# Hybrid decoder layer on one core: the mask selection operand is made once for all groups and reloaded, squares are added on VectorE, B is copied ahead of the masks, z is evaluated in pairs, the tap norm gets a lower priority

## Chip, cores and metric

The kernel runs on one core of a Trainium2 chip. The metric is the device time of one execution in microseconds (us). Before the change it is 1996.78 us, the median of three runs (1994.49 to 1999.12).

## The reference, cut to what matters

One layer with D_MODEL = 1024, SEQ = 1024, BATCH = 1, all in float32. The change touches the state-space branch (SSD) and the way the taps of the convolution branch are normalised:

```python
u = h @ w_in                         # -> GLU | z | x, B, C | dt | gate_a | gate_b
y_a = silu(layer_norm(causal_dwconv(a * sigmoid(g), 31 taps))) @ w_conv_out
...
# SSD: 32 heads in 4 groups of 8, head size 64, state 128, chunks of L = 128
a_cs = cumsum(dt * a_head)                           # within a chunk
decay = exp(a_cs[l] - a_cs[s]) where l >= s          # per head
cb = C @ B^T                                         # per group and chunk
y_diag = (cb * decay) @ (x * dt)
states, prev = scan over chunks of B^T @ (decay_states * x * dt)
y = y_diag + exp(a_cs) * (C @ prev) + x * d_skip
yg = y * silu(z)
y_b = yg * rsqrt(mean(yg^2 over the group)) * norm_w @ w_ssm_out
...
h = LN(alpha*h + (sigmoid(gate_a)*y_a + sigmoid(gate_b)*y_b) @ w_o)
h = LN(alpha*h + ConvFFN(h))
```

## The kernel before

Every large product is done with three TensorE (PE) products of 128x512 in the fp32r type (lines 187 to 189, `mm3`): each operand is split into a rounded part and a rest, ScalarE (ACT) writes the first and VectorE (DVE) the second (`weights`, lines 163 and 164; `split_to`, lines 203 and 204). SyncE (SP) issues the loads of the weights, GpSimd (POOL) issues some of the other DMAs. The sequence is worked on in two halves of 512 positions (`hh` = 0, 1); each goes through `mixers` and `combine`, then comes the output projection, and the ConvFFN follows for both.

`mixers` runs over the four SSD groups `g`. For a group it projects the columns of B, C and x, and passes each through `conv4` (line 429: three multiply-adds on DVE). Then it finishes the norm of the group before (`done`), projects two pairs of GLU columns, and calls `ssd_group`. `conv31` gets a low priority: its 30 multiply-adds of 128x512 for each of 8 channel tiles (line 474, `c`) are the filler that the planner puts between other work on DVE.

`ssd_group` runs over four chunks `c`. In a chunk PE makes `px` (x transposed, line 520) and `pb` (B transposed, line 523, and C times B, line 524, in one bank). POOL makes `au` (line 526), the differences' moving operand, 128 x (8 heads x 128): `seg_mv` of the chunk times the 0/1 choice `head_of` of the group's heads. PE makes the 8 masks' exponents with `seg_st` as weights and `au` as moving operand in two banks `pg` (line 535), ACT turns them into masks `m` (lines 543, 544), DVE multiplies them by `cbm` (line 558). `po` (line 563) is the part from the state, `pn` (line 567) the state's increment from `bt` (B transposed, copied by ACT in line 557) and `xsd`; DVE updates the state (lines 571, 574); `py` (line 577) is the part within the chunk. These banks, named `sm` in the profile, rotate through four; seven are taken in a chunk, so that a `pg` takes a bank which an earlier product's reader must have freed. The projections use four other banks, `acc`.

After the chunks, `z_gate` projects z in four tiles, ACT evaluates Silu on each; DVE forms y (lines 592, 596); ACT squares it, POOL adds the squares into `ss` (line 602). `normed` then sums them on PE (`pick`, line 607), takes the root (line 612) and the reciprocal (line 613), sends the row through DRAM (POOL DMAs, lines 615 and 616) and multiplies y by it (line 619), and splits it into `yT`.

`combine` projects the second gate and the second half of the SSD output (weights `w_gb`, `w_sp`) in turn, and beside them normalises the taps: loads `cc` from `c_scr`, adds them on POOL into `mean` (line 705), PE averages over partitions (line 707), and so on until `sT`, which the projection `w_co` needs. This stands under `tc.high_priority(offset=900)`.

The order on each engine is fixed when the kernel is built: a planner lays all instructions out on a timeline of its own, by priority (`tc.high_priority`) and by its own estimates of durations, and each engine then runs its list strictly in that order. An edit of one line so moves the instructions of all engines around it. `au`, `m`, `bt`, `xs`, `xsd` have one buffer each.

Of the kernel before, what the change touches and what calls it, by code (L numbers as in the profile page):

```python
# [8 lines left out]
F32 = mybir.dt.float32  # L9
F32R = mybir.dt.float32r  # L10
AF = mybir.ActivationFunctionType
ALU = mybir.AluOpType
# [42 lines left out]
def kernel(  # L55
# [30 lines left out]
    def bank(which):  # L86
        n_ps[0] += 1
        pl, tag = (pacc, "acc") if which else (psm, "sm")
        return pl.tile([P, 512], F32, tag=tag, name=f"{tag}{n_ps[0]}")
# [22 lines left out]
        axis=AX.X,  # L112
        op=ALU.add,
    )
    kind = const.tile([P, 4], F32, name="kind")
    V.tensor_reduce(
        out=kind, in_=ident.rearrange("p (g k h) -> p k g h", k=4, h=8), axis=AX.XY, op=ALU.add
# [34 lines left out]
    c_scr = [dram.tile([8, P, HALF], F32, name=f"c_scr{i}") for i in range(2)]  # L152
    g_scr = [dram.tile([8, P, HALF], F32, name=f"g_scr{i}") for i in range(2)]
    e_scr = [dram.tile([P, HALF], F32, name=f"e_scr{i}") for i in range(2)]
    r_scr = [dram.tile([GROUPS, HALF], F32, name=f"r_scr{i}") for i in range(2)]
    y_scr = [dram.tile([8, P, HALF], F32, name=f"y_scr{i}") for i in range(2)]

# [33 lines left out]
    def project(ps, w, xs):  # L191
        for k in range(KD):
            mm3(
                ps,
                lambda i: w[:, i, k * P : (k + 1) * P],
                lambda i: xs[:, i, k, :],
                k == 0,
                k == KD - 1,
            )
# [285 lines left out]
    def z_gate(pl, hh, hT, g):  # L485

        zs = []
        for i in range(4):
            ps = bank(1)
            project(ps, weights(wz[4 * g + i], f"z{hh}_{g}_{i}"), hT)  # L490
            z = pl.tile([P, HALF], F32, tag="zs", bufs=5, name=f"zs{hh}_{g}_{i}")
            A.activation(out=z, in_=ps, func=AF.Silu)
            zs.append(z)
        return zs

    def ssd_group(pl, hh, g, xT, BT, CT, gate):
        S = states[g]
        h8 = slice(8 * g, 8 * g + 8)
        acc = pl.tile([P, 4, HALF], F32, tag="ys", name=f"ys{hh}_{g}")
        ev = e_scr[hh].rearrange("(g k i j) t -> g k j i t", k=4, j=2, i=4)  # L500
        for j in range(2):
            G.dma_start(acc[j * HP : (j + 1) * HP], ev[g, 0, j].partition_broadcast(HP))

        def heads(t):
            return t.rearrange("p (h q) -> p h q", h=8)

        def per_head(t):
            return t.unsqueeze(2).to_broadcast([P, 8, HP])

        def by_tile(t):  # L510
            return t.rearrange("p (i t) -> p i t", i=4)

        for c in range(4):
            nm = f"{hh}_{g}_{c}"
            cs = slice(c * P, (c + 1) * P)
            first = hh == 0 and c == 0
            last = hh == 1 and c == 3
            px = bank(0)
            for i in range(4):
                TE.transpose(px[:, i * P : (i + 1) * P], xT[i][:, cs], ident)  # L520
            pb = bank(0)
            if not last:
                TE.transpose(pb[:, :P], BT[:, cs], ident)
            TE.matmul(pb[:, P : 2 * P], BT[:, cs], CT[:, cs], start=True, stop=True)
            au = pl.tile([P, 8, P], F32R, tag="au", name=f"au{nm}")
            G.tensor_tensor(  # L526
                out=au,
                in0=seg_mv[:, c, :].unsqueeze(1).to_broadcast([P, 8, P]),
                in1=head_of[:, g, :].unsqueeze(2).to_broadcast([P, 8, P]),
                op=ALU.mult,  # L530
            )
            m = pl.tile([P, 8, P], F32, tag="m", name=f"m{nm}")
            for q in range(2):
                pg = bank(0)
                TE.matmul(  # L535
                    pg,
                    seg_st[:, c, :],
                    au[:, 4 * q : 4 * q + 4, :].rearrange("p h l -> p (h l)"),
                    start=True,
                    stop=True,  # L540
                )
                mq = m[:, 4 * q : 4 * q + 4, :].rearrange("p h l -> p (h l)")
                A.activation(out=mq, in_=pg, func=AF.Relu)
                A.activation(out=mq, in_=mq, func=AF.Exp, scale=-1.0)
            cbm = pl.tile([P, P], F32, tag="cbm", name=f"cbm{nm}")
            V.tensor_mul(cbm, pb[:, P : 2 * P], upper)
            xs = pl.tile([P, HALF], F32, tag="xs", name=f"xs{nm}")
            V.tensor_tensor(
                out=heads(xs), in0=heads(px), in1=per_head(dts[0][:, c, h8]), op=ALU.mult
            )  # L550
            if not last:
                xsd = pl.tile([P, HALF], F32, tag="xsd", name=f"xsd{nm}")
                V.tensor_tensor(
                    out=heads(xsd), in0=heads(px), in1=per_head(dts[1][:, c, h8]), op=ALU.mult
                )
                bt = pl.tile([P, P], F32, tag="bt", name=f"bt{nm}")
                A.copy(bt, pb[:, :P])
            V.tensor_tensor(out=m, in0=m, in1=cbm.unsqueeze(1).to_broadcast([P, 8, P]), op=ALU.mult)  # L558
            if not first:
                po = bank(0)  # L560
                for i in range(4):
                    ts = slice(i * P, (i + 1) * P)
                    TE.matmul(po[:, ts], S[:, ts], CT[:, cs], start=True, stop=True)
                V.tensor_tensor(out=acc[:, :, cs], in0=by_tile(po), in1=acc[:, :, cs], op=ALU.mult)
            if not last:
                pn = bank(0)
                TE.matmul(pn, bt, xsd, start=True, stop=True)
                if first:
                    V.tensor_copy(S, pn)
                else:  # L570
                    V.tensor_tensor(
                        out=heads(S), in0=heads(S), in1=per_head(edc[:, 1, c, h8]), op=ALU.mult
                    )
                    V.tensor_add(S, S, pn)
            py = bank(0)
            for h in range(8):
                TE.matmul(
                    py[h % 2 * HP : (h % 2 + 1) * HP, h // 2 * P : (h // 2 + 1) * P],
                    xs[:, h * HP : (h + 1) * HP],
                    m[:, h, :],  # L580
                    start=True,
                    stop=True,
                )
            if first:
                A.copy(acc[:, :, cs], by_tile(py))
            else:
                V.tensor_tensor(out=acc[:, :, cs], in0=acc[:, :, cs], in1=by_tile(py), op=ALU.add)
        zs = gate()
        ss = pl.tile([P, HALF], F32, tag="ss", name=f"ss{hh}_{g}")
        for i, y in enumerate(xT):  # L590
            k = 4 * g + i
            V.scalar_tensor_tensor(
                out=y, in0=y, scalar=nskip[:, 1, k : k + 1], in1=acc[:, i, :],
                op0=ALU.mult, op1=ALU.add,
            )
            V.tensor_mul(y, y, zs[i])
            if i == 0:
                A.activation(out=ss, in_=y, func=AF.Square)
            else:
                sq = pl.tile([P, HALF], F32, tag="yo", bufs=2, name=f"sq{hh}_{g}_{i}")  # L600
                A.activation(out=sq, in_=y, func=AF.Square)
                G.tensor_add(ss, ss, sq)

        def normed(yT):
            pm = bank(0)
            for c in range(4):
                TE.matmul(
                    pm[:4, :P], pick[:, c, :], ss[:, c * P : (c + 1) * P],
                    start=c == 0, stop=c == 3,
                )  # L610
            r = pl.tile([4, P], F32, tag="rr", name=f"rr{hh}_{g}")
            A.activation(out=r, in_=pm[:4, :P], func=AF.Sqrt, bias=eps[:4], scale=1.0 / HALF)
            V.reciprocal(out=r, in_=r)
            rd = r_scr[hh][g]
            G.dma_start(rd.rearrange("(c t) -> c t", c=4), r)
            G.dma_start(ss, rd.partition_broadcast(P))
            for i, y in enumerate(xT):
                k = 4 * g + i
                V.scalar_tensor_tensor(  # L619
                    out=y, in0=y, scalar=nskip[:, 0, k : k + 1], in1=ss,  # L620
                    op0=ALU.mult, op1=ALU.mult,
                )
                split_to(yT, (g % 2) * 4 + i, y)

        return normed
# [40 lines left out]
    def combine(hh, hT, yT):  # L666

        with pool(f"comb{hh}") as pl:
# [11 lines left out]
            for j in range(8):  # L680
# [8 lines left out]
                V.tensor_add(m, ya, ps)  # L689
                V.tensor_mul(m, m, gb)  # L690
                mb.append(m)
            with tc.high_priority(offset=900):
                cs = []
                for i in range(8):
                    c = pl.tile([P, HALF], F32, tag=f"c{i}", name=f"cc{hh}_{i}")
# [652 lines left out]
```

## Time and profile before

| what | value |
|---|---|
| median of three runs | 1996.78 us |
| the profiled execution's own time | 1997.45 us |
| its span, first to last instruction | 1995.7 us |
| mean granted TensorE clock | 0.997 |
| stage `mixers`, half 0 | about 80 to 516 us of the span |
| stage `combine`, half 0 | about 516 to 660 us |
| stage `mixers`, half 1 | about 750 to 1180 us |
| stage `combine`, half 1 | about 1180 to 1310 us |
| ConvFFN | about 1310 us to the end |

The profile's page gives busy time by engine, the span in 40 slices, the chain of work that ended last, and groups of instructions. In a group's row stand the line, the engine, the operation, the tiles as written<-read, the shape, the count, then the busy time in us and the mean ns of one, then the idle time of its engine just before them and what ended it. A "wait" of PE is idle time between two of its matmuls, put down to what released it.

### The profile page before, as it was taken

To read this page: it belongs to the slowest core of one execution; us is meant where nothing else is said; L and a number is where in the kernel's file an instruction comes from. 1 tells how busy PE (TensorE), PEld (TensorE's weight loads), DVE (VectorE), ACT (ScalarE), POOL (GpSimd) and SP (SyncE) were. 2 spreads that over 40 slices of the span, in tenths; PEclk is the share of its full clock that TensorE was granted. 3 is DMA by queue.
4 is the path that set the end of the run, shared out by engine and by line. 5 is a ranking of instruction groups with operands and counts; after the bars stand their busy time and mean duration, and the time that the engine had idled before them with its cause. 6 is when DMAs were issued, how large, how long until landed. Compare 5 with 4: busy or idle time off the path is not lost.

```text
span 1995.7 us, 24843 instructions
## 1 busy us (share of the span) xinstructions
PE 1947.5 (98%) x9240; PEld 1592.9 (80%) x9240; DVE 1701.1 (85%) x2230; ACT 1052.9 (53%) x1483; POOL 237.4 (12%) x201
## 2 busy tenths in 40 slices
PE   7999999999999999999999999999999999999998
PEld 6887777877788887788777878887878888888886
DVE  7899999989565879999999967578998888778768
ACT  5566767454453266667654646256554544553442
POOL 1112121101400001111210132001000000011000
PEclk9999999999999999999999999999999999999999
DMA  6324232523544642324243354476443232268573
GB/s 218 111 65 121 73 117 79 164 81 115 175 127 155 240 140 77 102 84 117 80 132 116 100 185 127 132 279 241 170 148 116 101 113 104 102 215 272 181 248 111
DMA packets 99241, 281.15 MB, mean 141 GB/s; under 512 B 11728, under 2 KB 11760, under 8 KB 99120
## 3 DMA queue, kind: packets, MB, share of 16 engines
q1 hardware_dynamic: 87840, 244.68, 36.9%
q0 software_dynamic: 8976, 30.69, 5.1%
q10 hardware_dynamic: 2304, 4.20, 0.6%
q8 instruction: 72, 1.18, 0.2%
q14 instruction: 49, 0.40, 0.1%
HBM read 229.44 MB, written 50.09 MB: 140 GB/s over the span
## 4 chain that ended last, share of the span: by engine, by line
PE 64%; DVE 27%; issue 5%; DMA 2%; ACT 1%; POOL 1%; SPq 0%; DVEq 0%; POOLq 0%; ACTq 0%
PE acc L189 16%; PE acc L187 16%; PE acc L188 16%; DVE c L474 11%; PE sm L187 3%; PE sm L189 3%; PE sm L188 3%; DVE xbc L429 2%; DVE w_c L164 1%; PE acc L411 1%; DVE w_z L164 1%; DMA ss<-r_scr 1%; DVE m L558 1%; DVE xbc L619 1%; POOL mean L705 1%
## 5 line engine op out<-in xcount | busy, mean ns | idle before, releaser
L474 DVE SCALAR_TENSOR_TENSOR c<-v,pc,c 128x512 f32<-128x512 f32 x480 | 385.2, 832 | 5.5 <-ACT c L463 4.3
L187 PE MATMUL acc<-hT,w_c 128*128 128x512 f32 x352 | 141.6, 402 | 0.0
L189 PE MATMUL acc<-hT,w_c 128*128 128x512 f32 x352 | 138.5, 394 | 0.0
L188 PE MATMUL acc<-hT,w_c 128*128 128x512 f32 x352 | 137.9, 392 | 0.0
L526 POOL TENSOR_TENSOR au<-seg_mv,head_of 128x1024 fp32r<-128x1024 f32 x32 | 79.8, 2494 | 374.0 <-PE sm L535 373.9
L429 DVE SCALAR_TENSOR_TENSOR xbc<-u,pc,xbc 128x512 f32<-128x512 f32 x144 | 112.3, 794 | 0.5 <-ACT xbc L427 0.4
L987 DVE SCALAR_TENSOR_TENSOR fo<-u,pc,fo 128x1024 f32<-128x1024 f32 x88 | 111.4, 1286 | 0.4 <-ACT fo L983 0.4
L187 PE MATMUL acc<-h1s,w_s 128*128 128x512 f32 x264 | 103.5, 392 | 2.3 <-ACT u L971 2.3
L188 PE MATMUL acc<-hT,w_z 128*128 128x512 f32 x256 | 103.7, 405 | 0.0
L189 PE MATMUL acc<-h1s,w_s 128*128 128x512 f32 x264 | 103.0, 390 | 0.0
L188 PE MATMUL acc<-h1s,w_s 128*128 128x512 f32 x264 | 102.7, 389 | 0.0
L187 PE MATMUL acc<-hT,w_z 128*128 128x512 f32 x256 | 101.7, 397 | 0.0
L189 PE MATMUL acc<-hT,w_z 128*128 128x512 f32 x256 | 101.6, 397 | 0.0
L1126 ACT CAST w_dn<-dr 128x1024 fp32r<-128x1024 f32 (+1 forms) x73 | 61.0, 843 | 69.8 <-DVE dr L1056 33.3
L1127 DVE TENSOR_TENSOR w_dn<-dr,w_dn 128x1024 fp32r<-128x1024 f32 (+1 forms) x73 | 70.1, 968 | 13.5 <-ACT w_dn L1126 13.2
L188 PEld LDWEIGHTS acc<-hT,w_c 128*128 128x128 f32 x352 | 66.1, 188 | 15.7 <-issue 2.4
L187 PEld LDWEIGHTS acc<-hT,w_c 128*128 128x128 f32 x352 | 66.2, 188 | 15.3 <-issue 2.4
L189 PEld LDWEIGHTS acc<-hT,w_c 128*128 128x128 f32 x352 | 66.1, 188 | 14.5 <-issue 0.8
L163 ACT CAST w_c<-st_c 128x1024 fp32r<-128x1024 f32 x48 | 50.2, 1045 | 51.6 <-PE acc L189 32.5
L187 PE MATMUL sm<-h1b,w_s 128*128 128x512 f32 x176 | 69.1, 393 | 0.0
L188 PE MATMUL sm<-h1b,w_s 128*128 128x512 f32 x176 | 69.0, 392 | 0.0
L189 PE MATMUL sm<-h1b,w_s 128*128 128x512 f32 x176 | 69.0, 392 | 0.0
(372 smaller groups left out, 5708.3 us busy)
## 6 DMA issues: line engine op xcount, KB each, us to landing
st_c<-wcol SPq DMA_DIRECT2D x50, 512.0 KB, 3.5
st_z<-wz SPq DMA_DIRECT2D x32, 512.0 KB, 3.4
st_wo<-wo SPq DMA_DIRECT2D x24, 512.0 KB, 4.1
ra<-wup SPq DMA_DIRECT2D x22, 512.0 KB, 3.5
rb<-wup SPq DMA_DIRECT2D x22, 512.0 KB, 3.5
t_scr<-fo POOLq DMA_DIRECT2D x22, 512.0 KB, 3.4
dr<-t_scr SPq DMA_DIRECT2D x44, 256.0 KB, 3.8
dr<-wdown SPq DMA_DIRECT2D x38, 256.0 KB, 4.5
```

Source lines behind the costliest of these rows:

```text
L163: A.copy(w[:, 0, :], st)
L164: (eng or V).tensor_tensor(out=w[:, 1, :], in0=st, in1=w[:, 0, :].bitcast(F32), op=ALU.subtract)
L187: TE.matmul(ps, wa(0), xa(0), start=start, stop=False, skip_group_check=more)
L188: TE.matmul(ps, wa(0), xa(1), start=False, stop=False, skip_group_check=more)
L189: TE.matmul(ps, wa(1), xa(0), start=False, stop=stop, skip_group_check=more)
L411: TE.matmul(ps[:, ts], w[:, i, k * P : (k + 1) * P], hT[:, j, k, ts], start=n == 0 and k == 0, stop=n == 2 and k == KD - 1,)
L429: V.scalar_tensor_tensor(out=o, in0=u[:, k : k + HALF], scalar=pc[:, wc + k : wc + k + 1], in1=o, op0=ALU.mult, op1=ALU.add,)
L474: V.scalar_tensor_tensor(out=accs[i], in0=v[:, k : k + HALF], scalar=pc[:, wc + k : wc + k + 1], in1=accs[i], op0=ALU.mult, op1=ALU.add,)
L526: G.tensor_tensor(out=au, in0=seg_mv[:, c, :].unsqueeze(1).to_broadcast([P, 8, P]), in1=head_of[:, g, :].unsqueeze(2).to_broadcast([P, 8, P]),
L987: V.scalar_tensor_tensor(out=o, in0=u[:, k : k + T], scalar=pc[:, wc + k : wc + k + 1], in1=o, op0=ALU.mult, op1=ALU.add,)
L1126: A.copy(w[:, 0, cs], src)
L1127: V.tensor_tensor(out=w[:, 1, cs], in0=src, in1=w[:, 0, cs].bitcast(F32), op=ALU.subtract)
```

## The change

Five edits, all in `mixers` and `combine`. A tile `lanes` holds two sums of the 0/1 choice: `head_all` (which of the 8 heads in any group) and `group_of` (which group). `au` is now made with `head_all`, which is the same for all groups, so POOL makes it for group 0 alone and writes it to DRAM (`au_scr`); the three other groups load it. The choice of the group moves into the weights: ACT makes `sg` from `seg_st` and `group_of`, and PE uses `sg` where it used `seg_st`. `bt` is copied right after B's transposition, before C times B is written to the same bank. The adds into `ss` go to DVE. z's projections are evaluated two at a time. The tap norm's priority goes from 900 to 300.

```diff
+    lanes = statep.tile([P, 16], F32, name="lanes")
+    head_all, group_of = lanes[:, :8], lanes[:, 8:12]
+    V.tensor_reduce(
+        out=head_all, in_=head_of.rearrange("p g h -> p h g"), axis=AX.X, op=ALU.add
+    )
+    V.tensor_reduce(out=group_of, in_=head_of, axis=AX.X, op=ALU.add)
...
+    au_scr = [
+        [dram.tile([P, 8 * P], F32R, name=f"au_scr{i}_{c}") for c in range(4)] for i in range(2)
+    ]
...
-        for i in range(4):
-            ps = bank(1)
-            project(ps, weights(wz[4 * g + i], f"z{hh}_{g}_{i}"), hT)
-            z = pl.tile([P, HALF], F32, tag="zs", bufs=5, name=f"zs{hh}_{g}_{i}")
-            A.activation(out=z, in_=ps, func=AF.Silu)
-            zs.append(z)
+        for i in range(0, 4, 2):
+            pss = [bank(1) for _ in range(2)]
+            for k, ps in enumerate(pss):
+                project(ps, weights(wz[4 * g + i + k], f"z{hh}_{g}_{i + k}"), hT)
+            for k, ps in enumerate(pss):
+                z = pl.tile([P, HALF], F32, tag="zs", bufs=5, name=f"zs{hh}_{g}_{i + k}")
+                A.activation(out=z, in_=ps, func=AF.Silu)
+                zs.append(z)
...
                 TE.transpose(pb[:, :P], BT[:, cs], ident)
+                bt = pl.tile([P, P], F32, tag="bt", name=f"bt{nm}")
+                A.copy(bt, pb[:, :P])
             TE.matmul(pb[:, P : 2 * P], BT[:, cs], CT[:, cs], start=True, stop=True)
             au = pl.tile([P, 8, P], F32R, tag="au", name=f"au{nm}")
-            G.tensor_tensor(
-                out=au,
-                in0=seg_mv[:, c, :].unsqueeze(1).to_broadcast([P, 8, P]),
-                in1=head_of[:, g, :].unsqueeze(2).to_broadcast([P, 8, P]),
-                op=ALU.mult,
-            )
+            if g == 0:
+                G.tensor_tensor(
+                    out=au,
+                    in0=seg_mv[:, c, :].unsqueeze(1).to_broadcast([P, 8, P]),
+                    in1=head_all.unsqueeze(2).to_broadcast([P, 8, P]),
+                    op=ALU.mult,
+                )
+                G.dma_start(au_scr[hh][c], au.rearrange("p h l -> p (h l)"))
+            else:
+                G.dma_start(au.rearrange("p h l -> p (h l)"), au_scr[hh][c])
+            sg = pl.tile([P, P], F32R, tag="sg", name=f"sg{nm}")
+            A.mul(sg, seg_st[:, c, :].bitcast(F32), group_of[:, g : g + 1])
...
-                    seg_st[:, c, :],
+                    sg,
...
-                bt = pl.tile([P, P], F32, tag="bt", name=f"bt{nm}")
-                A.copy(bt, pb[:, :P])
...
                 A.activation(out=sq, in_=y, func=AF.Square)
-                G.tensor_add(ss, ss, sq)
+                V.tensor_add(ss, ss, sq)
...
-            with tc.high_priority(offset=900):
+            with tc.high_priority(offset=300):
```

The lists of the engines move from the middle of `mixers` to the end of `combine` in both halves; behind `combine` of half 1 they are as before. Three places follow. In the names of tiles stand the half, the group and the chunk (`au0_2_2` is half 0, group 2, chunk 2); line numbers of the changed kernel are larger by 9 to 17.

PE, half 0, group 2, from the last product of chunk 1 to the first masks' exponents of chunk 2, before:

```order
L577 MATMUL sm119_2519<-m0_2_1_2491,xs0_2_1_2502 64x128 x8
L520 MATMUL sm120_2529<-ident_75,xbc0_8_2154 128x128
L520 MATMUL sm120_2529<-ident_75,xbc0_9_2194 128x128
L520 MATMUL sm120_2529<-ident_75,xbc0_10_2234 128x128
L520 MATMUL sm120_2529<-ident_75,xbc0_11_2274 128x128
L523 MATMUL sm121_2534<-ident_75,xbc0_18_2074 128x128
L524 MATMUL sm121_2534<-xbc0_22_2114,xbc0_18_2074 128x128
L535 MATMUL sm122_2540<-au0_2_2_2537,seg_st_137 128x512
```

The same place in the changed kernel:

```order
L594 MATMUL sm119_2554<-m0_2_1_2528,xs0_2_1_2539 64x128 x8
L531 MATMUL sm120_2564<-ident_75,xbc0_8_2185 128x128
L531 MATMUL sm120_2564<-ident_75,xbc0_9_2225 128x128
L531 MATMUL sm120_2564<-ident_75,xbc0_10_2265 128x128
L531 MATMUL sm120_2564<-ident_75,xbc0_11_2305 128x128
L534 MATMUL sm121_2569<-ident_75,xbc0_18_2105 128x128
L554 MATMUL sm122_2579<-au0_2_2_2574,sg0_2_2_2576 128x512
```

C times B has left this block. It comes 20 projection matmuls later, just ahead of the second masks' exponents (here with the projection row before it and the row after it):

```order
L198 MATMUL acc143_3077<-hT0_214,w_c0_31_3080 128x512
L537 MATMUL sm121_2569<-xbc0_22_2145,xbc0_18_2105 128x128
L554 MATMUL sm123_2583<-au0_2_2_2574,sg0_2_2_2576 128x512
L196 MATMUL acc143_3077<-hT0_214,w_c0_31_3080 128x512
L197 MATMUL acc143_3077<-hT0_214,w_c0_31_3080 128x512
```

So between the transposition of B and C times B there is now the time in which ACT copies `bt`.

POOL, half 0, from the norm's two DMAs of group 0 to the end of group 1, before (`au` is made by POOL, `ss` added by POOL):

```order
L615 DMA r_scr0_199<-rr0_0_1493 4x128
L616 DMA ss0_0_1162<-r_scr0_199 128x512
L526 TENSOR_TENSOR au0_1_1_1694<-seg_mv_136,head_of_104 128x1024
L526 TENSOR_TENSOR au0_1_2_1742<-seg_mv_136,head_of_104 128x1024
L526 TENSOR_TENSOR au0_1_3_1790<-seg_mv_136,head_of_104 128x1024
L526 TENSOR_TENSOR au0_2_0_2448<-seg_mv_136,head_of_104 128x1024
L502 DMA ys0_2_2437<-e_scr0_197 64x4x512 x2
L602 TENSOR_TENSOR ss0_1_1958<-ss0_1_1958,sq0_1_1_1964 128x512
```

The same stretch in the changed kernel:

```order
L632 DMA r_scr0_210<-rr0_0_1516 4x128
L633 DMA ss0_0_1185<-r_scr0_210 128x512
L548 DMA au0_1_1_1721<-au_scr0_1_203 128x1024
L548 DMA au0_1_2_1771<-au_scr0_2_204 128x1024
L548 DMA au0_1_3_1821<-au_scr0_3_205 128x1024
L548 DMA au0_2_0_2481<-au_scr0_0_202 128x1024
L513 DMA ys0_2_2468<-e_scr0_200 64x4x512 x2
```

Loads stand where products stood, in the same places of the list, and the adds are gone from it.

PE, half 0, the sum of squares of the last group, before (among the last projections of `mixers`):

```order
L187 MATMUL acc196_4151<-hT0_203,w_gt0_7_4154 128x512
L188 MATMUL acc196_4151<-hT0_203,w_gt0_7_4154 128x512
L607 MATMUL sm190_3964<-ss0_3_3813,pick_117 4x128 x4
L189 MATMUL acc196_4151<-hT0_203,w_gt0_7_4154 128x512
L187 MATMUL acc196_4151<-hT0_203,w_gt0_7_4154 128x512
```

In the changed kernel, between the first two gate projections of `combine`:

```order
L197 MATMUL acc197_4235<-hT0_214,w_gb0_0_4238 128x512
L198 MATMUL acc197_4235<-hT0_214,w_gb0_0_4238 128x512
L624 MATMUL sm190_4011<-ss0_3_3860,pick_120 4x128 x4
L196 MATMUL acc198_4267<-hT0_214,w_gb0_1_4270 128x512
L197 MATMUL acc198_4267<-hT0_214,w_gb0_1_4270 128x512
```

The sum stands 43 projection matmuls later. The product `w_sp0_0`, the first that needs this group's `yT`, is cut in two there: 12 matmuls on the half of `yT` that is already there, the 24 of `w_gb0_2`, then the other 12. Between the sum and these other 12 stand 60 matmuls of 128x512 now; before, 67 and the first 12 of `w_sp0_0` stood between. In half 1 it is 54 now, 59 before.

## The prediction

> **What bounds the kernel now.** First the page: busy times, then the 40 slices, then the chain that ended last.
>
> ```profile
> span 1995.7 us, 24843 instructions
> PE 1947.5 (98%) x9240; PEld 1592.9 (80%) x9240; DVE 1701.1 (85%) x2230; ACT 1052.9 (53%) x1483; POOL 237.4 (12%) x201
> PE   7999999999999999999999999999999999999998
> DVE  7899999989565879999999967578998888778768
> PE 64%; DVE 27%; issue 5%; DMA 2%; ACT 1%; POOL 1%; SPq 0%; DVEq 0%; POOLq 0%; ACTq 0%
> ```
>
> PE is busy nearly throughout, and in slices 3 to 8 and 16 to 23, the two `mixers`, DVE is full as well. The chain alternates between these two. How much PE can gain at all is read by stage (busy us of PE, PEld, DVE, ACT, POOL in each stretch):
>
> ```profile
> 80.00:516.00 436.00, 427.01 (x2128) 342.65 (x2127) 418.22 (x547) 260.48 (x386) 64.36 (x42) 1.00 0.33 103
> 516.00:660.00 144.00, 140.48 (x609) 114.84 (x609) 88.58 (x110) 56.64 (x72) 21.60 (x14) 0.99 0.52 171
> 750.00:1180.00 430.00, 422.48 (x2122) 341.17 (x2121) 418.29 (x544) 252.57 (x349) 69.21 (x41) 1.00 0.34 104
> 1180.00:1310.00 130.00, 128.94 (x565) 105.53 (x564) 80.05 (x96) 59.66 (x75) 22.51 (x14) 1.00 0.49 157
> 1550.00:1600.00 50.00, 50.00 (x221) 41.15 (x220) 42.85 (x50) 24.28 (x29) 1.61 (x3) 1.00 0.31 111
> ```
>
> The last row is ConvFFN, where PE never waits: 50.00 / 221 = 0.226 us for each 128x512 matmul, the unit for distances below. PE idles 9.0 + 7.5 = 16.5 us in the `mixers` and 3.5 + 1.1 = 4.6 us in `combine`. The change adds and removes no matmul, so some 21 us, 1.1%, is all that it can win. What PE waits for there:
>
> ```profile
> PE sm L535 <- DVE state L574: 5.3, 5, 1.7
> PE sm L707 <- POOL mean L705: 4.6, 2, 3.5
> PE sm L567 <- ACT bt L557: 4.1, 3, 1.8
> PE acc L189 <- DVE w_ga L164: 2.4, 1, 2.4
> PE sm L535 <- DVE state L569: 1.6, 1, 1.6
> PE sm L563 <- DVE xsd L553: 1.5, 1, 1.5
> PE acc L189 <- DVE w_so L164: 1.3, 1, 1.3
> ```
>
> Without `mean` these are 5.3 + 4.1 + 2.4 + 1.6 + 1.5 + 1.3 = 16.2 us, the 16.5 of the windows. All but `bt` name a DVE that came late.
>
> **POOL's adds and products, taken away.** POOL makes `au` only for group 0 (8 of 32) and adds no squares. What POOL's work costs DVE shows where they meet:
>
> ```profile
> L474 DVE SCALAR_TENSOR_TENSOR c<-v,pc,c x480: 641/741/2391, 76.2 to 1163.9; 128x512 f32<-128x512 f32 x160
> L474 DVE SCALAR_TENSOR_TENSOR c<-v,pc,c 128x512 f32<-128x512 f32 x480 | 385.2, 832 | 5.5 <-ACT c L463 4.3
> L526 POOL TENSOR_TENSOR au<-seg_mv,head_of 128x1024 fp32r<-128x1024 f32 x32 | 79.8, 2494 | 374.0 <-PE sm L535 373.9
> L602 POOL TENSOR_TENSOR ss<-ss,sq 128x512 f32<-128x512 f32 x24 | 41.1, 1712 | 93.5 <-ACT sq L601 92.4
> 98.14 1.40 DVE L474 SCALAR_TENSOR_TENSOR c<-v,pc,c 128x512 f32<-128x512 f32 x2
> 100.60 3.05 DVE L474 SCALAR_TENSOR_TENSOR c<-v,pc,c 128x512 f32<-128x512 f32 x2
> 100.27 2.17 POOL L526 TENSOR_TENSOR au<-seg_mv,head_of 128x1024 fp32r<-128x1024 f32 x1 [14.62 <-PE sm L535]
> ```
>
> The same two multiply-adds take 1.40 us alone and 3.05 beside an `au`. Over all, line 474's mean of 832 ns stands over a median of 741: 480 x 0.091 = 43.7 us lost in this line alone, beside 79.8 + 41.1 = 120.9 us of these two POOL groups. Removed are 24/32 x 79.8 + 41.1 = 101 us of them, so at least 43.7 x 101/120.9 = 36 us of DVE come back. The Trainium skill ("SBUF — State Buffer", Who interferes with whom) says that a VectorE instruction with two inputs in SBUF and a reading GpSimd instruction exclude each other for a whole instruction; by it up to 101 us would come back, the trace says some 36, and the time below is the same by both, since PE is what it can free.
>
> DVE takes over 24 adds of 128x512 in SBUF, priced by line 596, the same form:
>
> ```profile
> L596 DVE TENSOR_TENSOR xbc<-xbc,zs 128x512 f32<-128x512 f32 x32 | 20.7, 699 | 0.0
> L557 ACT COPY bt<-sm x28: 242/266/274, 87.3 to 1118.7; 128x128 f32<-128x128 f32 x28
> ```
>
> 24 x 0.70 = 17 us. Each add now waits on DVE for ACT's square, with DVE's list behind it; weight splits and taps stand between in the new list, so I take no wait, and 24 x 0.63 = 15 us if ACT's square is always just being made. DVE's balance is -36 + 17 = -19 us of 836 us (-4 at the worst), a little more than the 16.5 us by which PE was kept waiting. The two small sums for `lanes` lie in the start, before x arrives.
>
> **New order of a chunk.** `pg` takes the bank that the state's increment of the chunk before held (DVE line 574 frees it). From `pn` to the next `pg` the old lists leave 3.9 us at least (counting matmuls in units of 0.226), five times under 6; the new ones 7.8 at least. `bt` is copied ahead of the masks instead of behind them, so its 4.1 us go; in exchange C times B now waits for that copy: 20 matmuls, 4.5 us, for a copy of 0.27 us on an ACT that is 60% busy (260.48 of 436). From the second `pg` to `py`, the room for masks, it is 7.9 us at least now, 7.3 before, and mostly 2 us more than before. From the transpositions to `pn`, the room for xs and xsd, it is 5.4 us at least and mostly 1 us less than before. What that takes:
>
> ```profile
> 109.45 0.66 PE L520 MATMUL sm<-ident,xbc 128*128 128x128 f32 x4
> 112.82 0.67 DVE L553 TENSOR_TENSOR xsd<-sm,wds 128x512 f32<-128x512 f32 x1
> ```
>
> 113.49 - 110.11 = 3.4 us with a full DVE, so 5.4 covers it. ACT gets 32 `sg` (as `bt`, 32 x 0.27 = 8.5 us) and six table switches by its list; it has room for both.
>
> Of the 16.2 us I take three quarters as gone, **12.2 us**: none at the least, if each wait only changes its place, and 16.2 at the most.
>
> **The reloads.** 24 loads of 512 KB and 8 stores. What such DMAs of POOL's queue take:
>
> ```profile
> t_scr<-fo POOLq DMA_DIRECT2D x22, 512.0 KB, 3.4
> ys<-e_scr POOLq DMA_DIRECT2D x16, 512.0 KB, 6.7
> L616 POOL DMA_DIRECT2D ss<-r_scr x8: 587/592/604, 177.6 to 1172.6; - x8
> 167.00 1.04 PE L607 MATMUL sm<-ss,pick 128*4 128x128 f32 x8
> 177.57 0.59 POOL L616 DMA_DIRECT2D ss<-r_scr  x1 [1.56 <-PE sm L535]
> ```
>
> A load is issued once the second `pg` has read the old `au`, and needed at the next `pg`, at least 9.8 us later by the new lists: 0.6 to issue and 3.4 to 6.7 to land fit in, so it costs 0. Chunk 1's load also stands behind the norm's two DMAs: `pick` at 167.0 us, `ss` issued by 178.2, then 4.0 to 7.3, is 15 to 18.5 us after `pick`; its `pg` is 19.1 (half 0) and 18.4 us behind `pick`. That fits barely. Waiting loads hold only POOL's queue, where r_scr and the next `ys` stand.
>
> **The exit to combine.** The norm's chain of the last group, half 0 and half 1:
>
> ```profile
> 494.99 1.04 PE L607 MATMUL sm<-ss,pick 128*4 128x128 f32 x8
> 509.15 2.74 DVE L619 SCALAR_TENSOR_TENSOR xbc<-xbc,nskip,ss 128x512 f32<-128x512 f32 x4 [6.22 <-DMA ss<-r_scr]
> 511.81 2.49 DVE L204 TENSOR_TENSOR yT<-xbc,yT 128x512 fp32r<-128x512 f32 x4
> 529.04 1.65 PE sm L707 x2
> 1164.35 1.04 PE L607 MATMUL sm<-ss,pick 128*4 128x128 f32 x8
> 1180.02 2.49 DVE L204 TENSOR_TENSOR yT<-xbc,yT 128x512 fp32r<-128x512 f32 x4
> ```
>
> The first rest of `yT` is there at 511.81 + 0.68 - 494.99 = 17.5 us after `pick` and at 16.4 in half 1. The new list needs it after 1.0 + 60 x 0.226 = 14.6 and 1.0 + 54 x 0.226 = 13.2 us: new waits of 2.9 and 3.2 us. `mean` is ready 34.1 us after `pick`, 0.8 more with the two `yb` loads now issued ahead; the new list asks for it 139 matmuls after `pick`, 1.0 + 31.4 + the 2.9 just lost = 35.3. So its 4.6 us go (in half 1, 133 matmuls, likewise). Lower priority buys 4.6 and the later `pick` costs 6.1: **+1.5 us**. z in pairs moves no matmul off PE; I take 0.
>
> **Sum.** -12.2 + 1.5 = -10.7 us against the profiled execution's 1997.45 us (span 1995.7), or against the median of 1996.78, which is 0.67 lower: 1986.1. I forecast **1986.1 us**.
>
> **Rivals.**
>
> 1. *The waits only change their place.* PE would meet DVE or ACT at C times B and at `pn`. If 28 copies of `bt` each come 0.4 us late, 11 us return: 1997. For it: 5.4 us of room for xs and xsd, and two engines full at once. Against it: DVE gets 19 us back, and the room for masks and state grows. Within 0.2%.
>
> 2. *Slower: chunk 1's load comes late.* If DVE, which is full, holds each POOL DMA as it holds `au` (1896 ns at best, 7598 at worst, see below), say by 2.5 us, the three in a row (two in group 2, where `au` stands ahead of `ss`) bring `au` up to 7.5 us later, 22 to 26 us after `pick`, where 17 to 19 are there: 5 us of PE in each of four places (groups 1 and 2 of both halves; group 3 has over 30 us). The other loads then need 9.8 against 9.8. It decides from some 1 us a DMA upward; +20: 2006.
>
> ```profile
> L526 POOL TENSOR_TENSOR au<-seg_mv,head_of x32: 1896/2110/7598, 69.0 to 1118.4; 128x1024 fp32r<-128x1024 f32 x32
> ```
>
> Against it, the norm's eight DMAs are issued in 587 to 604 ns beside the same full DVE. The Trainium skill (same page, SBUF: two separate sides) tells of this trap, descriptors of a GpSimd DMA locked out by VectorE; it says 620 ns may become 3100, and names two-port copies, which these adds are not; by the trace's 604 ns it does not happen here.
>
> 3. *All waits go*, 16.2, and the new `yT` waits don't come: 16.2 + 4.6 = 20.8 less, 1976. DVE's 19 us and more speak for it, the lists at the exit against it.
>
> **How the numbers follow.** Forecast (1979 to 1991) 0.50; rival 1 (1991 to 1999) 0.24; rival 2 (1999 to 2010) 0.15; rival 3 (below 1979) 0.11. About 0.2%, 4 us, is what a measurement can tell from no change. Faster by that is below 1992.8: 0.50 + 0.11 and 0.05 of rival 1, 0.66; within: 0.18; slower: 0.16. The range of 8 in 10 leaves out half of rival 3 and the upper half of rival 2: 1976 to 2003.
>
> **What would show it.** In the changed profile: line 474's successor with a mean near 760 ns; POOL's `au` x8; PE idle in the `mixers` down from 16.5 to about 4 us; waits of PE for `state` gone; PE waiting some 3 us for `yT` at each `w_sp0` and not for `mean`. Wrong would be: PE waits for `au` loads, for `bt` at C times B, or for `xsd`, or DVE waiting for ACT's squares.

## The result, and the profile after

The changed kernel takes 1967.62 us (median of four runs, 1966.87 to 1969.11), the kernel before 1997.95 beside it: a ratio of 0.9851, 95% interval 0.9834 to 0.9868. The forecast was 1986.1 within 1976 to 2003. The sign was right, the gain nearly three times the forecast, and the time lies below the range.

First the page of the changed kernel: span, busy times, the slices of PE and DVE, the chain that ended last.

```profile
span 1966.0 us, 24887 instructions
PE 1938.1 (99%) x9240; PEld 1591.8 (81%) x9240; DVE 1666.4 (85%) x2256; ACT 1069.9 (54%) x1521; POOL 153.0 (8%) x185
...
PE   7999999999999999999999999999999999999997
...
DVE  7899999999666879999999967588998887878868
...
PE 95%; DVE 3%; issue 1%; DMA 1%; ACT 0%; SPq 0%; DVEq 0%; ACTq 0%
```

The chain, 64% PE and 27% DVE before, is now 95% PE and 3% DVE: PE's own work decides the time. The span fell by 29.7 us. PE's idle time fell from 1995.7 - 1947.5 = 48.2 to 27.9 us, 20.3 less; the other 9.4 us came off PE's **busy** time (1947.5 to 1938.1), although it runs the same 9240 matmuls.

Now the `mixers` by stage, in equal stretches, first of the kernel before, then of the changed one (PE, PEld, DVE, ACT, POOL with their counts, granted clock, DMA share, GB/s):

```profile
80.00:510.00 430.00, 421.01 (x2102) 337.66 (x2101) 412.22 (x539) 255.18 (x379) 64.31 (x41) 1.00 0.33 103
740.00:1160.00 420.00, 412.48 (x2079) 333.53 (x2078) 414.58 (x541) 251.04 (x346) 68.75 (x41) 1.00 0.34 103
```

```profile
80.00:510.00 430.00, 430.00 (x2153) 347.70 (x2152) 400.79 (x560) 270.39 (x406) 22.71 (x32) 1.00 0.40 125
740.00:1160.00 420.00, 420.00 (x2127) 341.77 (x2126) 395.91 (x555) 263.00 (x368) 19.84 (x30) 1.00 0.40 127
```

PE idles for no measurable time in either stage, where the forecast left about 4 us of 16.5. In the same 430 us PE starts 51 matmuls more, in the 420 us 48 more; at 430/2153 = 0.2 us each that is 10 us a stage, a little more than the 9.0 and 7.5 us of idle time that had been visible.

A count by place in the list is sharper than one by time. Here are the last row of `w_gt`, which closes the projections of `mixers`, and the first row of `w_wo`, the output projection behind `combine`, in half 0 and in half 1, before and then in the changed kernel (start, duration, engine, line):

```profile
500.19 0.39 PE L189 MATMUL acc<-hT,w_gt 128*128 128x512 f32 x1
638.21 0.39 PE L187 MATMUL acc<-w_wo,mixT 128*128 128x512 f32 x1
1163.58 0.39 PE L189 MATMUL acc<-hT,w_gt 128*128 128x512 f32 x1
1298.96 0.39 PE L187 MATMUL acc<-w_wo,mixT 128*128 128x512 f32 x1
```

```profile
487.79 0.39 PE L198 MATMUL acc<-hT,w_gt 128*128 128x512 f32 x1
621.60 0.39 PE L196 MATMUL acc<-w_wo,mixT 128*128 128x512 f32 x1
1135.80 0.39 PE L198 MATMUL acc<-hT,w_gt 128*128 128x512 f32 x1
1269.61 0.39 PE L196 MATMUL acc<-w_wo,mixT 128*128 128x512 f32 x1
```

The four places come 12.4, 16.6, 27.8 and 29.4 us earlier. Of the first 12.4 us, 1.0 is the sum of squares, which now stands behind that row. So each `mixers` won some 11 us, and the two `combine` 5.2 and 1.6 us, where PE had idled for 3.5 and 1.1 us.

All waits of PE that the view of waits shows (engine, bank, line <- releaser: us, times, longest):

```profile
PE sm L222 <- DVE x L273: 13.7, 2, 12.4
PE acc L196 <- ACT u L988: 2.3, 2, 1.2
PE acc L196 <- ACT first L926: 0.9, 1, 0.9
PE acc L196 <- DVE r L782: 0.9, 1, 0.9
PE acc L410 <- ACT hT L228: 0.2, 1, 0.2
```

These are the start, the output projection and the ConvFFN, as before. Every wait of the two stages that the view lists is gone: `state`, `bt`, `xsd`, `w_ga`, `w_so`, and `mean`; none for `yT` has come. The groups that the change touches:

```profile
L483 DVE SCALAR_TENSOR_TENSOR c<-v,pc,c 128x512 f32<-128x512 f32 x480 | 347.6, 752 | 3.6 <-ACT c L472 2.9
L619 DVE TENSOR_TENSOR ss<-ss,sq 128x512 f32<-128x512 f32 x24 | 16.4, 683 | 0.2
L540 POOL TENSOR_TENSOR au<-seg_mv,lanes 128x1024 fp32r<-128x1024 f32 x8 | 16.0, 1999 | 79.2 <-PE sm L554 74.8 <-DMA au_scr<-au 4.4
L548 POOL DMA_DIRECT2D au<-au_scr x24 | 13.1, 544 | 369.3 <-PE sm L554 313.1 <-PE sm L537 53.5 <-PE acc L198 2.3
au<-au_scr POOLq DMA_DIRECT2D x24, 512.0 KB, 4.0
```

Line 483 is the old line 474: 752 ns in the mean, 37.6 us less in all. The adds cost DVE 16.4 us, with 0.2 us of idle time ahead of them. The loads of `au` are issued in 544 ns and land in 4.0 us.

### The profile page after: what moved, and what is told of

Read it like the earlier page. It is cut to its first block, busy times and chain, and to the rows that moved or that the text cites. A ratio compares the mean times of both kernels' runs of the same rounds, so it can differ in the third digit from the quotient of the medians.

```text
span 1966.0 us, 24887 instructions
## 1 busy us (share of the span) xinstructions
PE 1938.1 (99%) x9240; PEld 1591.8 (81%) x9240; DVE 1666.4 (85%) x2256; ACT 1069.9 (54%) x1521; POOL 153.0 (8%) x185
## 4 chain that ended last, share of the span: by engine, by line
PE 95%; DVE 3%; issue 1%; DMA 1%; ACT 0%; SPq 0%; DVEq 0%; ACTq 0%
PE acc L198 25%; PE acc L196 25%; PE acc L197 25%; PE sm L197 4%; PE sm L196 4%; PE sm L198 4%; PE sm L594 2%; PE sm L580 1%; PE sm L584 1%; PE acc L420 1%; PE sm L531 1%; PE sm L554 1%; DVE rows L270 1%; DVE rows L273 0%; PE acc L410 0%
## 5 line engine op out<-in xcount | busy, mean ns | idle before, releaser
L483 DVE SCALAR_TENSOR_TENSOR c<-v,pc,c 128x512 f32<-128x512 f32 x480 | 347.6, 752 | 3.6 <-ACT c L472 2.9
L438 DVE SCALAR_TENSOR_TENSOR xbc<-u,pc,xbc 128x512 f32<-128x512 f32 x144 | 106.4, 754 | 0.5 <-ACT xbc L436 0.4
L196 PE MATMUL acc<-h1b,w_ue 128*128 128x512 f32 x168 | 65.6, 390 | 0.9 <-ACT first L926 0.9
```

The costliest lines, as they stand in the source:

```text
L196: TE.matmul(ps, wa(0), xa(0), start=start, stop=False, skip_group_check=more)
L438: V.scalar_tensor_tensor(out=o, in0=u[:, k : k + HALF], scalar=pc[:, wc + k : wc + k + 1], in1=o, op0=ALU.mult, op1=ALU.add,)
L483: V.scalar_tensor_tensor(out=accs[i], in0=v[:, k : k + HALF], scalar=pc[:, wc + k : wc + k + 1], in1=accs[i], op0=ALU.mult, op1=ALU.add,)
```

## The experiments

Two theories stood against each other. **Contention**: POOL's instructions stretch DVE's beside them, DVE comes late, PE waits; less work on POOL is the whole gain. **Order**: the planner's new lists leave more room between producer and consumer, and whose work it is matters little. The runs were made on several chips, so each is compared with the kernel before on its own chip, by the ratio.

| run | what it is | median, us | ratio to before, 95% | DVE busy, us |
|---|---|---|---|---|
| do_bt | before + early copy of B | 1987.19 | 0.9954 (0.9938 to 0.9970) | 1694.4 |
| do_reload | before + reload of au | 1975.33 | 0.9889 (0.9872 to 0.9906) | 1668.7 |
| do_ss | before + squares on DVE | 1974.65 | 0.9888 (0.9870 to 0.9906) | 1692.9 |
| do_tap | before + tap norm later | 2001.24 | 1.0014 (1.0003 to 1.0026) | 1701.8 |
| un_bt | changed, copy of B late | 1972.99 | 0.9867 (0.9843 to 0.9892) | 1664.7 |
| un_reload | changed, au on POOL | 1969.16 | 0.9848 (0.9833 to 0.9864) | 1687.3 |
| un_ss | changed, squares on POOL | 1970.15 | 0.9856 (0.9839 to 0.9873) | 1667.4 |
| un_tap | changed, tap norm early | 1968.08 | 0.9844 (0.9828 to 0.9859) | 1660.6 |
| do_dup | do_ss + 24 idle adds on POOL | 1996.76 | 0.9991 (0.9979 to 1.0003) | 1717.3 |
| dup_ss | changed + 24 idle adds on POOL | 1971.52 | 0.9863 (0.9841 to 0.9885) | 1687.5 |
| dup_au | changed + 24 products on POOL | 1978.86 | 0.9902 (0.9875 to 0.9930) | 1702.0 |
| dup_both | changed + both | 2000.60 | 1.0015 (1.0003 to 1.0027) | 1723.7 |
| do_ms | do_ss + 48 fills on POOL | 1973.03 | 0.9874 (0.9860 to 0.9889) | 1693.3 |
| do_cp | do_ss + 24 copies on POOL | 1983.09 | 0.9921 (0.9904 to 0.9937) | 1701.9 |
| pool_both | changed, au and squares on POOL | 1986.35 | 0.9939 (0.9924 to 0.9954) | 1698.4 |

### One edit at a time

do_bt moves two lines up:

```diff
                 TE.transpose(pb[:, :P], BT[:, cs], ident)
+                bt = pl.tile([P, P], F32, tag="bt", name=f"bt{nm}")
+                A.copy(bt, pb[:, :P])
...
-                bt = pl.tile([P, P], F32, tag="bt", name=f"bt{nm}")
-                A.copy(bt, pb[:, :P])
```

> The kernel before with one edit: B is copied right after its transposition. Theory relief (DVE wins because POOL no longer holds it, the order matters little): only the waits for bt go, 4 us, so -4 us or less against the kernel before. Theory order (the new lists give state, masks and B more room): most of the 16 us of waits in the mixers go, -12 to -20 us, although POOL's au and squares are as before and the multiply-adds of line 474 still take about 830 ns.

do_reload takes the part with `lanes`, `au_scr` and `sg`; its core:

```diff
+            if g == 0:
...
+                G.dma_start(au_scr[hh][c], au.rearrange("p h l -> p (h l)"))
+            else:
+                G.dma_start(au.rearrange("p h l -> p (h l)"), au_scr[hh][c])
...
-                    seg_st[:, c, :],
+                    sg,
```

> The kernel before with one edit: au is made with head_all for group 0 and reloaded for the others, the group chosen by sg. Theory relief: POOL's au fall from x32 to x8, some 30 us of DVE come back, the waits of PE for state, xsd and w_ga shrink, those for bt stay: -10 to -18 us. Theory order: waits stay within 4 us of the old ones, -5 us at most.

do_ss is one line:

```diff
-                G.tensor_add(ss, ss, sq)
+                V.tensor_add(ss, ss, sq)
```

> The kernel before with one edit: squares are added by VectorE. Theory relief: POOL's adds stretched DVE by about 25 us in all, the adds cost it 17 us, balance -8 us: -3 to -8 us on the time. If stretching by POOL costs nothing, DVE has 17 us more to do in two stages where it is full: +5 to +17 us.

do_tap:

```diff
-            with tc.high_priority(offset=900):
+            with tc.high_priority(offset=300):
```

> The kernel before with one edit: priority of the tap norm 900 to 300. All theories: the waits for mean (4.6 us) go. The step of the prediction that adds two waits for yT of about 3 us each gives +1.5 us; if those do not come, -4.6 us.

The copy of B alone won 0.46%, about 9 us: more than contention had allowed it, less than order had. PE's largest wait within the stages is now the state's increment waiting for `xsd`, a tile for which PE waited 1.5 us before:

```profile
PE sm L567 <- DVE xsd L555: 7.1, 4, 3.6
```

So, with POOL's work left on POOL, waits do change their place, as rival 1 of the prediction says. Each POOL edit alone won 1.1%, 22 us, more than any expectation above had allowed. The shares don't add up: 9 + 22 + 22 - 3 is 50, and all together give 30. The priority did not win its 4.6 us: it lost 0.14%. Its waits for `mean` and the first wait for `yT`:

```profile
PE sm L707 <- POOL mean L705: 5.8, 2, 4.4
PE acc L187 <- ACT yT L203: 1.3, 1, 1.3
```

Nothing was run for z in pairs: the lists of all engines with and without that edit are the same row for row, so it can't have a part in the time.

### One edit taken back

Each of un_bt, un_reload, un_ss and un_tap is the changed kernel without that part, the diffs above read backwards.

> The changed kernel with one edit undone: B is copied behind the masks again. Theory relief with a floor (either of the two POOL edits alone already gave 22 of 30 us; what bounds the rest is PE itself): PE still has its work in time because DVE is no longer held; +0 to +4 us against the changed kernel. Theory order: the copy alone gave 9 us, so +9 us.

> The changed kernel with one edit undone: POOL makes au for every group again. Relief with a floor: the adds on VectorE alone gave 22 us and B's copy 9, so most stays: +0 to +6 us. If the shares of the edits add up: +22 us.

> The changed kernel with one edit undone: POOL adds the squares again. Relief with a floor: the reload alone gave 22 us and B's copy 9: +0 to +6 us. If the shares add up: +22 us.

> The changed kernel with one edit undone: priority of the tap norm 300 to 900. If the priority takes away the waits for mean, they come back: +3 to +5 us. If, as in the kernel before, it gains nothing or costs 3 us: -3 to 0 us.

None of the four parts is missed when it alone is taken back: all four ratios lie within the changed kernel's interval (un_bt, the largest, 0.16% above its 0.9851). There is a floor, and one POOL edit with the copy of B and the tap norm is enough to reach it; by the chain, 95% PE, it is PE's own work. The two priorities of the tap norm give the same time, and in un_tap PE does not wait for `mean` either.

This still left both theories alive, since every edit but z's also reorders hundreds of rows. And do_ss spoke for order: its DVE is as full as before (415.6 of 430 us in half 0's `mixers`, 412.2 before), and yet PE's waits were nearly gone: it idles for 0.8 and 0.9 us in the two stretches, where 9.0 and 7.5 us stood before.

### The same lists, with and without POOL's work

So POOL's work was put back where no other engine's list notices it. Adds that nobody needs, behind the new add on DVE:

```diff
                 V.tensor_add(ss, ss, sq)
+                G.tensor_add(zs[i], zs[i], y)
```

> The kernel before with squares added by VectorE (do_ss, 1974.7 us), and 24 more adds of 128x512 on POOL beside them that nobody needs: the lists of PE, DVE, ACT and SP are those of do_ss row for row, POOL's work is that of the kernel before. Theory contention (POOL stretches DVE by some 25 us with these adds, and PE waits for it): the 22 us come back in large part, 1985 to 1998. Theory order (the lists that the planner made are what counts): 1975 to 1978.

All 22 us came back: the ratio is 0.9991 where do_ss has 0.9888. PE, DVE, ACT and SP run the same instructions in the same order in both; only POOL differs. For this edit contention holds and order falls. Busy times on the page of do_ss, then of do_dup:

```profile
PE 1941.4 (98%) x9240; PEld 1591.5 (81%) x9240; DVE 1692.9 (86%) x2254; ACT 1056.9 (54%) x1487; POOL 197.8 (10%) x177
```

```profile
PE 1945.2 (98%) x9240; PEld 1590.3 (80%) x9240; DVE 1717.3 (86%) x2254; ACT 1055.8 (53%) x1487; POOL 244.5 (12%) x201
```

The largest waits of PE in do_dup, without that of the start:

```profile
PE sm L567 <- ACT bt L557: 4.3, 3, 2.9
PE sm L708 <- POOL mean L706: 4.1, 2, 2.7
PE sm L535 <- DVE state L569: 3.5, 2, 2.5
PE sm L535 <- DVE state L574: 3.4, 5, 0.8
PE acc L189 <- DVE w_ga L164: 2.4, 1, 2.4
```

The same 2254 DVE instructions take 24.4 us longer, and the old waits are back, for `state`, `bt`, `w_ga` and `mean`. PE's busy time rises as well, by 3.8 us for the same matmuls: a part of each wait is booked as busy (how is told below, with the prediction's first step). ACT's `bt` and POOL's `mean` stand in this list although no edit touched them; which engine a wait names says who came last, not who made it late.

The same on the changed kernel, with one more product in place behind each load of `au`, or the adds, or both:

```diff
                 G.dma_start(au.rearrange("p h l -> p (h l)"), au_scr[hh][c])
+                G.tensor_tensor(
+                    out=au,
+                    in0=au.bitcast(F32),
+                    in1=head_all.unsqueeze(2).to_broadcast([P, 8, P]),
+                    op=ALU.mult,
+                )
```

> As dup_both with the 24 idle adds alone. Theory contention: some 25 us of DVE lost at the ends of the groups, 1975 to 1990. Theory order: 1968 to 1972.

> As dup_both with the multiplications alone (POOL's au x32 again, 24 of them in place behind the load). Theory contention: some 30 us of DVE lost, PE waits, 1978 to 1990. Theory order: 1968 to 1972.

> The changed kernel with POOL's old work put back beside the new: after each load of au POOL multiplies it once more in place by head_all (x24), and adds 24 squares that nobody needs. The lists of PE, DVE, ACT and SP are those of the changed kernel row for row. Theory contention: DVE loses its 46 us again and keeps the 17 us of adds, so PE waits more than in the kernel before: 1995 to 2010. Theory order: 1968 to 1975, since the lists leave room.

With POOL's old work back, all 30 us are gone and 3 more (1.0015). The row of the times is a curve: DVE longer by 21.1 us (dup_ss) costs 0.12% in the ratio, some 2 us and within the intervals; by 35.6 (dup_au) 0.51%, 10 us; by 57.3 (dup_both) 1.64%, 33 us. The time of dup_ss, 1971.5, by itself lies in the range of order; that the first 20 us cost so little would be DVE's own idle time (430 - 400.79 = 29 us in half 0's `mixers`, 420 - 395.91 = 24 in half 1's). The last 22 us cost PE nearly one for one. That would explain why the single edits did not add up, the first relief winning back the late part and the second only adding slack; it is argued from the curve, not tested. (The curve is one for fixed lists: do_reload and do_ss give the same time with DVE busy times 24 us apart.) Waits of PE in dup_both:

```profile
PE sm L560 <- issue: 5.8, 7, 1.9
PE sm L590 <- DVE xsd L578: 4.4, 3, 3.2
PE sm L631 <- DVE ss L625: 4.1, 5, 1.5
PE acc L197 <- DVE yT L213: 1.4, 1, 1.4
PE acc L196 <- ACT yT L212: 1.0, 1, 1.0
```

Line 560 reads `au`. Its 5.8 us are probably the experiment's own, since the product makes each load later by some 2 us, so dup_au and dup_both overstate contention by about that much; do_dup, whose adds nobody waits for, has no such fault. The waits for `yT` that the prediction feared at the exit are there, 2.4 us, once DVE is held again.

### What of POOL's work it is

In place of the idle adds of do_dup stand fills in do_ms, and copies in do_cp:

```diff
-                G.tensor_add(zs[i], zs[i], y)
+                for _ in range(2):
+                    G.memset(zs[i], 0.0)
```

```diff
-                G.tensor_add(zs[i], zs[i], y)
+                G.tensor_copy(zs[i], y)
```

> do_ss (1974.7 us) with 48 fills of 128x512 by a constant on POOL where do_dup has 24 adds; the lists of PE, DVE, ACT and SP are those of do_ss row for row. If an instruction of POOL that reads nothing does not hold DVE: 1974 to 1977. If any POOL instruction that writes to SBUF does: 1985 to 1997, as do_dup.

> do_ss with 24 copies of 128x512 on POOL (one operand read) where do_dup has 24 adds; the lists of the other engines are those of do_ss row for row. If one operand is enough to hold DVE: some 1985 to 1997. If it takes two: 1974 to 1978.

POOL's rows of do_ms, do_cp and do_dup:

```profile
L604 POOL MEMSET zs<- 128x512 f32 x48 | 23.8, 529 | 86.7 <-ACT ss L598 47.1 <-DVE xbc L596 38.9
```

```profile
L603 POOL COPY zs<-xbc 128x512 f32<-128x512 f32 x24 | 33.9, 1451 | 87.8 <-ACT ss L598 47.2 <-DVE xbc L596 40.6
```

```profile
L603 POOL TENSOR_TENSOR zs<-zs,xbc 128x512 f32<-128x512 f32 x24 | 50.6, 2136 | 87.9 <-ACT ss L598 47.3 <-DVE xbc L596 40.7
```

23.8 us of fills lengthen DVE by 0.4 us (1693.3 against 1692.9) and cost no time; 33.9 us of copies lengthen it by 9.0 and cost 0.33%; 50.6 us of adds lengthen it by 24.4 and cost 1.03%. The time of do_cp lies between its two expected ranges: one operand read is enough to hold DVE, though less than two do; writing alone does not. The three differ in POOL's time too, but per us of POOL the order is the same: 0.48 us of DVE for the adds, 0.27 for the copies, 0.02 for the fills. The Trainium skill ("SBUF — State Buffer", Who interferes with whom) says that a VectorE instruction with two SBUF inputs contends with a GpSimd instruction that reads SBUF, not with one that only writes it; these three runs agree.

### Order without relief

pool_both is the changed kernel with these two parts taken back:

```diff
-            if g == 0:
-                G.tensor_tensor(
+            G.tensor_tensor(
...
-                V.tensor_add(ss, ss, sq)
+                G.tensor_add(ss, ss, sq)
```

> The changed kernel with both POOL edits undone: POOL makes au for every group (with head_all; sg is kept) and adds the squares; B's copy, the pairs and the tap norm stay. Theory contention: as do_bt, 1984 to 1992, some 20 us above the changed kernel. Theory order: 1968 to 1973.

0.9939, where do_bt has 0.9954: with POOL's work on POOL, copy of B, `sg` and tap norm together give what the copy of B gives alone, and PE waits for `xsd` again (8.4 us). The lists here are again the planner's own, not those of the changed kernel. The new order is worth some 10 us while DVE is late, and 0.16% in the median, within the intervals, once it is not (un_bt). Why it helps a late DVE at all was not tested. By itself it does not bring the 30 us: pool_both wins 12 of them, and dup_both, with the changed kernel's order on every engine but POOL, wins nothing (though its DVE has the 24 adds to do as well).

## Why the prediction was wrong, step by step

| step | forecast, us | measured, us |
|---|---|---|
| waits inside the `mixers` and `combine`, shown by the view | -12.2 | -16.2 |
| exit to `combine` | +1.5 | -4.6 |
| PE's busy time | 0 | -9.4 |
| reloads, z in pairs | 0 | 0 |
| sum | -10.7 | -30.2 (span: -29.7) |

1. **"Some 21 us, 1.1%, is all that it can win"** failed first. It took PE's idle time for all of PE's lost time. Three rows of the kernel before show how a wait is booked (start, duration, engine, line, and the idle time that the view counts):

```profile
462.20 0.39 PE L188 MATMUL acc<-hT,w_gt 128*128 128x512 f32 x1
463.38 0.47 PE L535 MATMUL sm<-au,seg_st 128*128 128x512 f32 x1 [0.79 <-DVE state L574]
463.69 0.39 PE L189 MATMUL acc<-hT,w_gt 128*128 128x512 f32 x1
```

A matmul is drawn 0.39 us long, but the next one starts 0.23 us after it when nothing holds PE. From 462.20 to 463.69 two steps take 1.49 us, and should take 0.45: 1.04 us are lost, of which the view calls 0.79 a wait. A wait under 0.16 us it doesn't show at all. So some 21 us of visible idle time in these stages stood for about 30, which the count of matmuls in a stretch shows (51 and 48 more in the `mixers`) and the busy share of 98% hides.

Of the 9.4 us of busy time, some 3.4 are the granted clock. Just after the two longest waits of the kernel before, 3.5 us for `mean` and 2.4 us for `w_ga`, the clock (third number from the end) is halved for 3.41 us, and the matmuls start 0.43 us apart in place of 0.23:

```profile
529.50:532.91 3.41, 3.41 (x8) 2.27 (x7) 2.75 (x5) 1.46 (x3) 0.16 (x1) 0.50 0.49 153
833.29:836.70 3.41, 3.41 (x9) 2.66 (x9) 3.41 (x5) 1.33 (x2) 0.00 (x0) 0.50 0.48 154
833.09 0.65 PE L189 MATMUL acc<-hT,w_ga 128*128 128x512 f32 x1 [2.44 <-DVE w_ga L164]
833.53 0.63 PE L187 MATMUL acc<-hT,w_ga 128*128 128x512 f32 x1
```

That is 2 x 3.41 x 0.5 = 3.4 us, all booked as busy. The changed kernel has no such stretch but in its last 6 us, as the kernel before has in its own. The halving does not follow every wait of this length: do_dup has it after 2.4 us for `w_ga`, and not after its 2.9 us for `bt`.

The Trainium skill ("Trainium Kernel Development and Optimization", Performance Expectations) calls matmul busy time a bad metric for how close a kernel is to roofline, because matmuls are pipelined. The rows above show this pipelining, 0.39 us drawn and 0.23 from start to start, and the prediction used busy time as a bound all the same.

2. **"Of the 16.2 us I take three quarters as gone"**: all are gone. The relief was under-sized: 36 us were a lower bound by one line, and the balance was drawn with it. Line 474 gave back 37.6 us (385.2 to 347.6) where 36 were forecast, and the adds cost 16.4 where 17 were. DVE's busy time fell by 34.7 us with the adds included, so all lines together got back 34.7 + 16.4 = 51 us. The balance was -35, not -19. That all waits go and not three quarters follows from there, as far as dup_au and dup_both show it: with POOL's work put back in part, or whole, the waits return in part, or whole.

3. **The exit, +1.5 us**, had the wrong sign. Pick, first product and first rest of `yT` in half 0, then half 1, of the changed kernel:

```profile
493.55 1.04 PE L624 MATMUL sm<-ss,pick 128*4 128x128 f32 x8
503.45 2.74 DVE L636 SCALAR_TENSOR_TENSOR xbc<-xbc,nskip,ss 128x512 f32<-128x512 f32 x4 [0.83 <-DMA ss<-r_scr]
506.11 2.49 DVE L213 TENSOR_TENSOR yT<-xbc,yT 128x512 fp32r<-128x512 f32 x4
...
1142.91 1.04 PE L624 MATMUL sm<-ss,pick 128*4 128x128 f32 x8
1154.60 2.49 DVE L213 TENSOR_TENSOR yT<-xbc,yT 128x512 fp32r<-128x512 f32 x4
```

The first rest stands 506.11 + 0.68 - 493.55 = 13.2 us after `pick`, in half 1 12.4, where the prediction carried over 17.5 and 16.4 from the old trace; 14.6 and 13.2 were there. It priced the chain at its old durations, and these did not hold. POOL's first DMA of the chain in half 0, before and now:

```profile
501.36 0.54 POOL L615 DMA_DIRECT2D r_scr<-rr  x1 [7.17 <-DVE rr L613]
497.63 0.51 POOL L632 DMA_DIRECT2D r_scr<-rr  x1 [50.34 <-DVE rr L630]
```

From `pick` to this DMA it takes 4.1 us now and 6.4 before, since DVE comes to the reciprocal sooner; from this DMA to the first product, mostly the two transfers, 5.8 now and 7.8 before. In half 1 the two parts shrank by 1.4 us, as ACT comes to the root sooner, and by 2.6 us. Why the transfers land sooner no run shows. The `mean` waits went through the relief of DVE, not through the priority: do_tap keeps them, un_tap has none, and with fixed lists they are 1.1 us in do_ss and 4.1 in do_dup.

4. **Reloads at 0, z in pairs at 0**: right. Rival 2 (held POOL DMAs) did not occur: 544 ns an issue. Rival 1 (waits change place) did not occur here, though it did in do_bt and pool_both. Rival 3, all waits go and no new ones come, was the case, at 0.11; its 20.8 us lacked the 9.4 of step 1.

The mechanism named, POOL beside a full DVE, was the right one; the three errors all pointed the same way, and the first of them also cut the range.

## What to carry to other kernels

Read lost time of a pipelined engine from start to start, or from the same place in its list, not from its idle time: here 20 us of visible idle were 30, 3.4 of them a halved clock. When two engines share a resource, the price is the longer busy time of the victim over all its lines, and what that costs depends on its slack: here the first 20 us were nearly free and the last 20 cost about one for one, so single edits neither add up nor subtract. To tell contention from order, put the suspected work back as work that nobody needs, and see that the other engines' lists stay the same. Here a one-line move of 24 adds to the full engine won 22 of the 30 us.

## What the runs showed of the hardware

- Beside a DVE that is 97% busy in the `mixers` (415.60 of 430 us in do_ss), a POOL add of 128x512 (2.1 us in do_dup) costs DVE 24.4/24 = 1.0 us, a copy (1.45 us) 0.4, a fill (0.53 us) less than 0.01. DVE's own add of the same size takes 0.68 us in the changed kernel: here POOL's help cost DVE more than doing the work itself.
- Issuing POOL's loads was not held by the full DVE: 544 ns in the mean over 24, 537 to 582 ns.
- In the kernel before, the two longest waits of PE in these stages (3.5 and 2.4 us) are each followed by 3.41 us at a granted clock of 0.50, in which matmuls of 128x512 start 0.43 us apart. In do_dup a wait of 2.9 us is not.
